# A streamed trunk of stick-breaking attention, sparse attention and two Strassen-style MLPs: second seed behind s3, its copies in tiles of their own, other times in the step planner, and x blocks through DRAM in 1 KB runs

## The chip, the core and the metric

The kernel runs on one core of a Trainium2 chip. The metric is the device time of one execution in microseconds (us): the median over the runs. TensorE (PE) multiplies, VectorE (DVE) and ScalarE (ACT) do elementwise work, GpSimd (POOL) and SyncE (SP) mainly issue DMAs here. All five run their own instruction streams in order and wait for one another through semaphores.

## The reference

256 tokens of width 2048 go through two residual layers; each is a mixer and then an MLP. What matters here is the MLP, which takes two thirds of the time:

```
for i in range(2):
    h = rms_norm(x, norm_mix[i])
    x = x + (stick_breaking_mixer(h, ...) if i == 0 else dsa_mixer(h, ...))
    h = rms_norm(x, norm_mlp[i])
    x = x + jnp.square(jax.nn.relu(h @ w_up[i])) @ w_down[i]     # 2048 -> 8192 -> 2048
```

All of it is float32. The mixers end in an output projection (out_proj) whose result is added to x.

## The kernel before, in words

**Weights and splits.** Weights stream from DRAM as blocks of 128 x 1024 float32 (256 rows of the matrix by 512 columns, 512 KB). Every block is one *item*. A load into a ring of six `wraw` tiles (L1777, queue of SP) is followed by a *split* into two float32r parts: ACT copies the block to `wh` (L1794), DVE subtracts it to get the rest `wl` (L1795). Each ring of parts has four tiles, so ACT may split an item once PE is done with the item four places earlier. The left operands are split likewise, and a product is the three partial products high x high, low x high, high x low: 12 matmuls for both token halves (a plain item, L855), or 6 for one half (a product of the set, L837).

**The MLP as pairs.** `mlp(l, next_col)` works on *pairs* of 512-column output groups, G and H. Each of the 16 pairs of a layer has eight weight blocks per column, and for all but the first (`up0`) four of the eight are replaced by two sets, a and b, of seven products each, in which sums of weight blocks (X, Y, Z, formed by DVE at L966, L969 and L978 and by a DMA that adds, issued by POOL at L973) meet sums of left blocks (`Sa`, `Sb` in the down pairs; the tile `Sx`, which the profile calls `half`, in the up pairs). So a pair is 14 products and 8 plain items, 14 x 6 + 8 x 12 = 180 matmuls. Their order on PE is written out: s1a . s1b s5a . s5b s6a s6b . s7a s7b s3a s3b . s2a s4a s2b s4b G0 G1 G2 G3; at the dots come the last items H0 to H3 of the pair before. 15 pairs of this kind run in each of the two MLPs, 30 in all.

**Seeds.** The products share sums. G's accumulator is a PSUM tile of two halves; s1, s6 and s7 add up in its second half. In `seeds(p, prior)` five small steps carry partial sums on: `first` (ACT, L1002) copies the second half to the first half of G after s1b; `second` (ACT, L1006) copies it to the first half of a tile U after s6b; `third` (ACT, L1009) copies it to the second half of U after s7b; `fourth` (DVE, L1013) opens the accumulator H and writes its first half, U subtracted from the product s5; `fifth` (DVE, L1016) writes its second half in the same way, and this is the **second seed**. s3a and s3b then add into H's first half, and H0 to H3 into both. The tile framework puts the waits in by whole tiles: a matmul into H waits for a write to H that stands before it in the program, whichever half it is.

**What sets the order of the side work.** The steps (seeds, sums, transposes, relu and square, DMAs) are put between the items by a planner, `Plan.run`, ahead of time. It walks over the items with costs written as numbers (A, V, MM for a split on ACT, on DVE and a matmul), with a latency per engine (`LAT`) and a latest start per step, and decides after which item each step is issued; the engines then run in that order. `done` holds a step back until an item has been issued, `needs` gives the item that must find it done.

**The way around DRAM.** A finished column of G or H is transposed by DVE in 32 x 32 blocks into a tile `y` (L926), written to DRAM by four DMAs (L934) and read back transposed (L942), in runs of 1 KB. At the end of a mixer, `add_residual` (L572) adds out_proj's result to x, and `turn` takes each of four x columns on a way of its own: L427 transposes, L435 writes in runs of 128 bytes, L440 reads, ACT (L471) and DVE (L476) form the high and low part of `xT`, the left operand of the MLP's first items. The places of these steps are fixed item counts (`later`).

Of the kernel before, what the change touches and what calls it, by code (L numbers as in the profile page):

```python
# [17 lines left out]
P = 128  # L18
# [24 lines left out]
NEAR = 5  # L43
DEEP = 3
ADD = True
# [49 lines left out]
class Plan:  # L95
# [3 lines left out]
    LAT = {"A": 0.25, "V": 0.25, "S": 2.6, "P": 3.5, "PE": 0.5}  # L99
    AHEAD = {"A": 1.2, "V": 2.0}  # L100

    def __init__(self, items, lead, bufs, raw):
        self.items, self.lead, self.bufs, self.raw = items, lead, bufs, raw
        self.steps = []
# [10 lines left out]
    def run(self, start, rings, extra=16):  # L115
# [30 lines left out]
        free = {"A": ideal[start], "V": ideal[start], "S": ideal[start]}  # L146
# [6 lines left out]
        self.own, self.loads = own, {}  # L153
        pe = ideal[start]
        late = 0.0

        def raw_free(k):
# [3 lines left out]
            t = lo.get(i)  # L161
# [51 lines left out]
        def place(s, i, t):  # L213
# [3 lines left out]
            if s.eng in "SP":  # L217
                b = max(free["S"], t)
                free["S"] = b + s.cost
                s.end = b + s.cost + self.LAT[s.eng]  # L220
            else:
                b = max(free[s.eng], t)
                s.end = free[s.eng] = b + s.cost
# [6 lines left out]
        for i in range(start, n + extra):  # L230
# [23 lines left out]
            while loaded < len(own):  # L254
# [32 lines left out]
            while more:  # L287
                more = False
                for s in todo[:60]:
# [6 lines left out]
                    else:  # L296
# [4 lines left out]
                        must = s.slot + late < pe + 1.5  # L301
                        if not must and (room < self.AHEAD[s.eng] or idle > 0.4
                                         and b > pe):
                            continue
# [21 lines left out]
def trunk(ctx, tc, x, x_t, gains_t, w_in_a, w_out_a, w_in_b, w_in_b_end, w_out_b, rel_bias, w_up, w_down, out):  # L326
# [92 lines left out]
    def turned(parts, whole=False, y=None):  # L419

        n = sum(part.shape[1] // P for part in parts)
        y = (tmp.tile([P, 8, P], F32, name="jx", bufs=3) if y is None else y)[:, :n, :]
# [36 lines left out]

    def turn_steps(c, col):  # L460
# [20 lines left out]
    def turn(c, col, wait):  # L481

        parts, high, low = turn_steps(c, col)

        def then(z):
            z = z.rearrange("p (t k) (a q) -> p t k a q", t=2, a=4)
# [3 lines left out]
        to_features(parts, any_tile, then, wait)  # L490
# [276 lines left out]
    def mlp(l, next_col):  # L767
# [119 lines left out]
        for i in range(6):  # L887
            add(up0, f"G{i}", f"H{i}")
        add(up0, "G6", "G7")
        before, tail = up0, ["H6", "H7"]  # L890
        for p in pairs:
            order = "s1a . s1b s5a . s5b s6a s6b . s7a s7b s3a s3b .".split()
            gaps = {4: (0, 1, 2, 3), 2: (1, 2)}[len(tail)]
            gap = 0
            for name in order:
                if name != ".":
                    add(p, name)
                    continue
                if gap in gaps:
                    add(before, tail.pop(0))  # L900
                gap += 1
            add(p, *"s2a s4a s2b s4b G0 G1 G2 G3".split())
# [15 lines left out]
        def turn(part, room):  # L918
            def f():
                if room.ring == "y":  # L920
                    room.tile = sec["pool"].tile([P, 4, 8, 32], F32, name="y", bufs=1)
                else:
                    room.tile = any_tile().rearrange("p n (b i) -> p (n b) i", b=4).rearrange(
                        "p (b n) i -> p b n i", b=4)
                for n, x in part():
                    keep(dve.transpose(room.tile[:, :, n, :], x.rearrange("p (k b i) -> p b k i",  # L926
                                                                          b=4, i=32)))
            return f

        def write(room):  # L930
            def f():
                room.d = drp.tile([4, 32, 4, 256], F32, name="tu", bufs=4)
                for a in range(4):
                    keep(nc.sync.dma_start(  # L934
                        room.d[:, :, a, :].rearrange("b j e -> j b e"),
                        room.tile[32 * a:32 * a + 32].rearrange("p b n i -> p b (n i)")))
            return f

        def read(room, d):
            def f():  # L940
                room.tile = any_tile().rearrange("p a e -> p (a e)")
                keep(nc.sync.dma_start(room.tile, d.d.rearrange("b j a e -> (b j) (a e)")))  # L942
            return f

        def by_token(z):
# [945 lines left out]
```

## Time and profile before

| | us |
|---|---|
| median of 3 runs (lowest, highest) | 2093.45 (2092.56, 2096.15) |
| the profiled execution, its own time | 2085.08 |
| its span, first to last instruction | 2083.4 |
| first mixer and the first items of the first MLP (0 to 416): PE busy | 413.9 |
| first MLP (416 to 1050): PE busy, DVE busy | 603.2, 563.2 |
| second mixer (1050 to 1404): PE busy | 354.0 |
| second MLP (1404 to 2084): PE busy, DVE busy | 644.7, 596.1 |

A row such as `wl<-wraw,wh` reads "tile written <- tiles read"; numbers of buffers are left out, so `acc` is any of the accumulators G and H, `aux` holds s5. Idle time of an engine that others do not wait for costs nothing; what has to be read is where PE stands, and what it stands for.

### The profile page before, as it was taken

To read this page: it belongs to the slowest core of one execution; us is meant where nothing else is said; L and a number is where in the kernel's file an instruction comes from. 1 tells how busy PE (TensorE), PEld (TensorE's weight loads), DVE (VectorE), ACT (ScalarE), POOL (GpSimd) and SP (SyncE) were. 2 spreads that over 40 slices of the span, in tenths; PEclk is the share of its full clock that TensorE was granted. 3 is DMA by queue.
4 is the path that set the end of the run, shared out by engine and by line. 5 is a ranking of instruction groups with operands and counts; after the bars stand their busy time and mean duration, and the time that the engine had idled before them with its cause. 6 is when DMAs were issued, how large, how long until landed. Compare 5 with 4: busy or idle time off the path is not lost. (4 is left out here: it accounts for less than half of the span.)

```text
span 2083.4 us, 25469 instructions
## 1 busy us (share of the span) xinstructions
PE 2015.8 (97%) x8858; PEld 1653.3 (79%) x8858; DVE 1747.8 (84%) x1921; ACT 1284.4 (62%) x1551; POOL 86.0 (4%) x131
## 2 busy tenths in 40 slices
PE   9999999999899999999999999999999999999999
PEld 7888888877777877887788788887777787778777
DVE  6779866799889889988885897669888898999886
ACT  6666655476566666666564566555666566676554
POOL 0000100002000000000000000000000000000000
PEclk9999999999999999999999999999999999999999
DMA  9777757878878877886677697587867788688774
GB/s 347 215 226 210 224 162 214 265 239 266 262 251 247 266 229 247 252 279 226 188 270 253 193 263 242 159 281 219 290 209 246 229 251 256 213 265 283 237 218 140
DMA packets 261537, 496.34 MB, mean 238 GB/s; under 512 B 121312, under 2 KB 150048, under 8 KB 261408
## 3 DMA queue, kind: packets, MB, share of 16 engines
q1 hardware_dynamic: 244720, 455.81, 66.1%
q0 software_dynamic: 8640, 31.46, 8.3%
q10 hardware_dynamic: 8048, 7.45, 1.1%
q8 instruction: 69, 1.13, 0.2%
q14 instruction: 60, 0.49, 0.1%
HBM read 457.36 MB, written 37.22 MB: 237 GB/s over the span
## 5 line engine op out<-in xcount | busy, mean ns | idle before, releaser
L1795 DVE TENSOR_TENSOR wl<-wraw,wh 128x1024 fp32r<-128x1024 f32 (+1 forms) x674 | 810.6, 1215 | 172.1 <-ACT wh L1794 162.5
L1794 ACT ACTIVATE wh<-wraw 128x1024 fp32r<-128x1024 f32 (+1 forms) x674 | 702.1, 1052 | 353.9 <-PE acc L855 111.4
L855 PE MATMUL acc<-wh,xT 128*128 128x512 f32 x1152 | 285.3, 390 | 2.8 <-DVE xT L476 2.8
L855 PE MATMUL acc<-wh,half 128*128 128x512 f32 x1016 | 256.4, 395 | 0.0
L855 PEld LDWEIGHTS acc<-wh,xT 128*128 128x128 f32 x1152 | 216.5, 188 | 48.5 <-DVE xT L476 3.4
L855 PEld LDWEIGHTS acc<-wh,half 128*128 128x128 f32 x1016 | 195.4, 192 | 41.7
L837 PE MATMUL acc<-wh,half 128*128 128x512 f32 x720 | 196.8, 396 | 16.3 <-DVE acc L1016 16.3
L558 PE MATMUL acc<-wh,xT 128*128 128x512 f32 x736 | 185.7, 392 | 0.0
L837 PEld LDWEIGHTS acc<-wh,half 128*128 128x128 f32 x720 | 136.3, 190 | 48.4 <-DVE acc L1016 19.7
L558 PEld LDWEIGHTS acc<-wh,xT 128*128 128x128 f32 x736 | 137.6, 188 | 30.0 <-issue 1.7
L855 PE MATMUL acc<-wl,xT 128*128 128x512 f32 x576 | 154.0, 389 | 0.0
L855 PE MATMUL acc<-wl,half 128*128 128x512 f32 x508 | 135.8, 389 | 0.0
L855 PEld LDWEIGHTS acc<-wl,xT 128*128 128x128 f32 x576 | 108.1, 188 | 22.5
L837 PE MATMUL acc<-wl,half 128*128 128x512 f32 x360 | 112.4, 394 | 1.7 <-DVE wl L1795 1.7
L855 PEld LDWEIGHTS acc<-wl,half 128*128 128x128 f32 x508 | 95.5, 188 | 20.0
L1794 ACT ACTIVATE wh<-Zb 128x1024 fp32r<-128x1024 f32 x60 | 63.3, 1056 | 63.2 <-PE acc L855 32.7
L558 PE MATMUL acc<-wl,xT 128*128 128x512 f32 x368 | 99.2, 391 | 0.0
L1795 DVE TENSOR_TENSOR wl<-Zb,wh 128x1024 fp32r<-128x1024 f32 x60 | 73.3, 1222 | 27.8 <-ACT wh L1794 27.0
L837 PE MATMUL acc<-wh,xT 128*128 128x512 f32 x336 | 89.8, 389 | 0.0
L837 PEld LDWEIGHTS acc<-wl,half 128*128 128x128 f32 x360 | 68.6, 191 | 16.7 <-DVE wl L1795 2.1
L558 PEld LDWEIGHTS acc<-wl,xT 128*128 128x128 f32 x368 | 68.9, 188 | 14.9 <-DVE wl L1795 0.3
L662 PE MATMUL acc<-wh,xT 128*128 128x512 f32 x320 | 79.7, 391 | 0.0
(296 smaller groups left out, 3022.1 us busy)
## 6 DMA issues: line engine op xcount, KB each, us to landing
wraw<-in_w_up_dram SPq DMA_DIRECT2D x228, 512.0 KB, 5.3
wraw<-in_w_down_dram SPq DMA_DIRECT2D x224, 512.0 KB, 5.0
wraw<-in_w_in_a_dram SPq DMA_DIRECT2D x88, 512.0 KB, 4.7
wraw<-in_w_in_b_dram SPq DMA_DIRECT2D x64, 512.0 KB, 4.6
jx<-tu SPq DMA_DIRECT2D x36, 512.0 KB, 6.2
wraw<-in_w_out_a_dram SPq DMA_DIRECT2D x32, 512.0 KB, 4.1
tu<-y SPq DMA_DIRECT2D x128, 128.0 KB, 4.0
wraw<-in_w_out_b_dram SPq DMA_DIRECT2D x32, 512.0 KB, 4.3
```

What stands on the lines that cost most here:

```text
L558: (keep if alone else pin)(pe.matmul(acc[t], L[:, KB * q + j, part, t * P:(t + 1) * P], wx[:, j, :], start=a and q == 0, stop=z and q == Q ...
L662: keep(pe.matmul(acc[:, t, :], L[:, KB * qs[i] + j, part, t * P:(t + 1) * P], wx[:, j, :], start=a and i == 0, stop=z and i == end - (last ...
L837: keep(pe.matmul(o, lhs(part, j), wx[:, j, :], start=a and opens, stop=z, skip_group_check=True))
L855: keep(pe.matmul(acc[:, t, :], L[:, KB * q + j, part, t * P:(t + 1) * P], wx[:, j, :], start=a and i == 0 and not self.sets, stop=z, skip_ ...
L1794: order(act.activation(wh[:, a], raw[:, a], AF.Copy))
L1795: order(dve.tensor_sub(wl[:, a], raw[:, a], wh[:, a].bitcast(F32)))
```

## The change

It has four parts.

1. **Seeds.** `fifth` also waits until s3b has been issued, so it stands behind s3 in the program. The copies of `second` and `third` go to tiles of their own, 128 x 512 from a ring of two, in place of two halves of one tile. `third` must be done by s2a, not by s4a.
2. **The planner's numbers.** Latencies are set to other values, SP's and POOL's transfers share one modelled set of DMA engines and have a time to issue each, and a step that reads what a DMA brings is not placed within 3 us (`SURE`) of the modelled landing unless it is due. The planner starts at item 4 of the MLP, not at item 8.
3. **x blocks.** `turn` uses the same layout as the MLP's columns: runs of 1 KB both ways. The fourth column's read and its two parts become steps of the planner (`last_column`), due at G6.
4. **The MLP's first items.** G0 H0 ... G4 H4 G5 G6 G7, with H5, H6, H7 at the dots of the next pair (before: up to H5 in turn, then G6 G7, with H6 and H7 at the dots).

The additions by DMA stay as they were (`ADD` is now a function that always answers True), as does every matmul, split and sum.

```
-ADD = True
+ADD = lambda p, s: True
...
-    LAT = {"A": 0.25, "V": 0.25, "S": 2.6, "P": 3.5, "PE": 0.5}
+    LAT = {"A": 1.5, "V": 2.0, "S": 2.0, "P": 3.0, "PE": 0.5}
+    SURE = 3.0
+    ISSUE = {"S": 0.33, "P": 1.2}
...
+        def transfer(queue, t, cost):
+            b = free[queue] = max(free[queue], t) + self.ISSUE[queue]
+            free["D"] = max(free["D"], b) + cost
+            return free["D"] + self.LAT[queue]
...
-                b = max(free["S"], f, pe - 10)
-                free["S"] = b + 1.5
-                landed[own[loaded]] = b + 1.5 + 2.6
+                landed[own[loaded]] = transfer("S", max(f, pe - 10), 1.6)
...
-                        if not must and (room < self.AHEAD[s.eng] or idle > 0.4
-                                         and b > pe):
+                        if not must and (room < self.AHEAD[s.eng] or idle > 0.4
+                                         and b > pe or b < landed_at + self.SURE):
...
     def turn(c, col, wait):
 
         parts, high, low = turn_steps(c, col)
+        y = y_view(any_tile())
+        for t in range(2):
+            turn_in(y, 4 * t, parts[t], lambda ins: None)
+
+        def write():
+            d = turn_write(y)
+            if c < 3:
+                later(3, read, d)
+            else:
+                handed.update(d=d, high=high, low=low)
...
-        to_features(parts, any_tile, then, wait)
+        later(1 + wait, write)
...
-        for i in range(6):
+        for i in range(5):
             add(up0, f"G{i}", f"H{i}")
-        add(up0, "G6", "G7")
-        before, tail = up0, ["H6", "H7"]
+        add(up0, "G5", "G6", "G7")
+        before, tail = up0, ["H5", "H6", "H7"]
...
             def second():
-                sec["U"] = sec["pool"].tile([P, 2, 512], F32, name="U", bufs=1)
-                keep(act.activation(sec["U"][:, 0, :], p.G[:, 1, :], AF.Copy))
+                p.two = sec["pool"].tile([P, 512], F32, name="U", bufs=2)
+                keep(act.activation(p.two, p.G[:, 1, :], AF.Copy))
 
             def third():
-                keep(act.activation(sec["U"][:, 1, :], p.G[:, 1, :], AF.Copy))
+                p.three = sec["pool"].tile([P, 512], F32, name="U", bufs=2)
+                keep(act.activation(p.three, p.G[:, 1, :], AF.Copy))
...
-            b = plan.step("A", 0.5, third, done(p, "s7b") + after(*prior.seed), needs("s4a"))
+            b = plan.step("A", 0.5, third, done(p, "s7b") + after(*prior.seed), needs("s2a"))
             a = plan.step("V", 0.6, fourth, done(p, "s5b") + after(a, prior.out["G"]), needs("s3a"))
-            p.seed = [a, plan.step("V", 0.6, fifth, after(a, b), needs("H0"))]
+            b = plan.step("V", 0.6, fifth, after(a, b) + done(p, "s3b"), needs("H0"))
+            p.seed = [a, b]
...
+        def last_column():
+
+            z = Room("jx")
+            b = plan.step("S", 1.5, read(z, lambda: handed["d"]), takes=z)
+            b = plan.step("A", 1.6, lambda: handed["high"](by_token(z.tile)), after(b), uses=[z])
+            plan.step("V", 2.1, lambda: handed["low"](by_token(z.tile)), after(b),
+                      [("mm", up0.by["G6"])], uses=[z])
...
-        for i, steps in plan.run(8, {"jx": 3, "y": 1}).items():
+        for i, steps in plan.run(4, {"jx": 3, "y": 1}).items():
```

Where the instructions stand is shown at three places of the first down pair, the third of the first MLP's 15 pairs, as each engine's program lists them (the times there are in the prediction). Numbers behind names tell tiles apart, `x3` stands for three alike, and the brackets name the engines whose semaphores an instruction waits for. Source lines of the changed kernel are some 30 to 45 higher: L1043 and L1046 are its fourth and fifth step, L882 and L900 its matmuls, L1835 its split on DVE.

PE before, from s3a (on `Sa`) over s3b (on `Sb`) to the plain item; `acc_4289` is H:

```order
L837 MATMUL acc_4289<-wh_4273,Sa_3136 128x512 [waits DVE_49,PE_49,Activation_49]
L837 MATMUL acc_4289<-wh_4273,Sa_3136 128x512 x3
L837 MATMUL acc_4289<-wl_4274,Sa_3136 128x512 x2
L837 MATMUL acc_4289<-wh_4293,Sb_3140 128x512 [waits DVE_49]
L837 MATMUL acc_4289<-wh_4293,Sb_3140 128x512 x3
L837 MATMUL acc_4289<-wl_4294,Sb_3140 128x512 x2
```

and the same place of the changed kernel, where H is `acc_4290`:

```order
L882 MATMUL acc_4290<-wh_4269,Sa_3148 128x512 [waits DVE_49,PE_49,Activation_49]
L882 MATMUL acc_4290<-wh_4269,Sa_3148 128x512 x3
L882 MATMUL acc_4290<-wl_4270,Sa_3148 128x512 x2
L882 MATMUL acc_4290<-wh_4294,Sb_3152 128x512 [waits Activation_49]
L882 MATMUL acc_4290<-wh_4294,Sb_3152 128x512 x3
L882 MATMUL acc_4290<-wl_4295,Sb_3152 128x512 [waits DVE_49]
```

The matmuls are the same; the first one of s3b no longer waits for DVE, only for ACT's part of its own weights.

DVE before, from the fourth step (L1013) to the split behind the fifth (L1016), at the same place:

```order
L1013 TENSOR_TENSOR acc_4289<-aux_4171,U_4266 128x512 [waits DVE_49]
L1795 TENSOR_TENSOR wl_4294<-wraw_4101,wh_4293 128x1024 [waits PE_49,Activation_49]
L978 TENSOR_TENSOR Za_3139<-Za_3139,wraw_4122 128x1024 [waits DMAHW5_49]
L1795 TENSOR_TENSOR wl_4307<-wraw_4103,wh_4306 128x1024 [waits DMAHW4_49,PE_49,Activation_49]
L1795 TENSOR_TENSOR wl_4319<-wraw_4122,wh_4318 128x1024 [waits PE_49,Activation_49]
L1016 TENSOR_TENSOR acc_4289<-aux_4171,U_4266 128x512 [waits PE_49,Activation_49]
L1795 TENSOR_TENSOR wl_4331<-Za_3139,wh_4330 128x1024 [waits Activation_49]
```

and of the changed kernel, where the fifth step is L1046:

```order
L1043 TENSOR_TENSOR acc_4290<-aux_4174,U_4265 128x512 [waits DVE_49]
L1007 TENSOR_TENSOR Za_3151<-Za_3151,wraw_4142 128x1024 [waits DMAHW6_49]
L1835 TENSOR_TENSOR wl_4295<-wraw_4107,wh_4294 128x1024 [waits PE_49,Activation_49]
...
L473 STREAM_TRANSPOSE y_4409<-acc_3909 128x1024 [waits DMAHW5_49,DMAHW6_49,DMAHW4_49,DMAHW3_49]
L1835 TENSOR_TENSOR wl_4412<-wraw_4337,wh_4411 128x1024 [waits DMAHW2_49,PE_49,Activation_49]
L995 TENSOR_TENSOR Xa_3149<-Ya_3150,wraw_4349 128x1024 [waits DMAHW3_49]
L1046 TENSOR_TENSOR acc_4290<-aux_4174,U_4317 128x512
```

The fifth step went from 5 rows behind the fourth to 17 rows behind it, past the next pair's first sum, and it waits for no other engine there. In the whole program it stands at 18 of 30 places with waits for PE and ACT before, and at 5 with a wait for PE now.

DVE at the start of the same pair before, where the low part of the left sum Sb (L1116) is formed:

```order
L969 TENSOR_TENSOR Za<-Xa,wraw 128x1024
L1795 TENSOR_TENSOR wl<-Xa,wh 128x1024
L1795 TENSOR_TENSOR wl<-wraw,wh 128x1024
L1101 TENSOR_TENSOR jx<-jx 128x2x4x32
L1102 TENSOR_TENSOR jx<-jx 128x2x4x32
L1103 TENSOR_TENSOR jx<-jx 128x2x4x32
L1104 TENSOR_TENSOR jx<-jx 128x2x4x32
L969 TENSOR_TENSOR Zb<-Xb,wraw 128x1024
L1795 TENSOR_TENSOR wl<-Xb,wh 128x1024
L1795 TENSOR_TENSOR wl<-Za,wh 128x1024
L1116 TENSOR_TENSOR Sb<-jx,Sb 128x1024
```

and of the changed kernel (L998 is L969, L1147 is L1116):

```order
L998 TENSOR_TENSOR Za<-Xa,wraw 128x1024
L1835 TENSOR_TENSOR wl<-wraw,wh 128x1024
L998 TENSOR_TENSOR Zb<-Xb,wraw 128x1024
L1835 TENSOR_TENSOR wl<-Xb,wh 128x1024
L1147 TENSOR_TENSOR Sb<-jx,Sb 128x1024
L1835 TENSOR_TENSOR wl<-Za,wh 128x1024
```

The four sums (L1101 to L1104) now stand ahead of this place, and the low part comes four rows behind Za, not ten.

More of the change, by code (lines that the diff above doesn't have):

```diff
@@ L43 @@
 NEAR = 5
+ORDER = "s1a . s1b s5a . s5b s6a s6b . s7a s7b s3a s3b . s2a s4a s2b s4b G0 G1 G2 G3"
 DEEP = 3
-ADD = True
+ADD = lambda p, s: True
 LEAD = 2
@@ L153, in run @@
         self.own, self.loads = own, {}
+        self.held = {index(a): index(b) for a, b in self.hold}
         pe = ideal[start]
         late = 0.0
+        def transfer(queue, t, cost):
+            b = free[queue] = max(free[queue], t) + self.ISSUE[queue]
+            free["D"] = max(free["D"], b) + cost
+            return free["D"] + self.LAT[queue]
         def raw_free(k):
@@ L160, in raw_free @@
             i = own[k - self.raw]
-            t = lo.get(i)
+            t = lo.get(self.held.get(i, i))
             if t is None:
@@ L301, in run @@
                         must = s.slot + late < pe + 1.5
+                        landed_at = max([x.end for kind, x in s.after
+                                         if kind == "step" and x.eng in "SP"] + [0.0])
                         if not must and (room < self.AHEAD[s.eng] or idle > 0.4
-                                         and b > pe):
+                                         and b > pe or b < landed_at + self.SURE):
                             continue
@@ L417, in later, with turned @@
         due[clock[0] + n].append(lambda: f(*a))
[L419 removed]
+    def turned(parts, whole=False):
         n = sum(part.shape[1] // P for part in parts)
[L422 removed]
+        y = tmp.tile([P, 8, P], F32, name="jx", bufs=3)[:, :n, :]
         m = 0
@@ L885, in add @@
             items.extend(p.by[name] for name in names)
-        for i in range(6):
+        for i in range(5):
             add(up0, f"G{i}", f"H{i}")
-        add(up0, "G6", "G7")
-        before, tail = up0, ["H6", "H7"]
+        add(up0, "G5", "G6", "G7")
+        before, tail = up0, ["H5", "H6", "H7"]
         for p in pairs:
[L892 to L895, printed above, removed]
+            for name in ORDER.split():
                 if name != ".":
                     add(p, name)
-                    continue
-                if gap in gaps:
+                elif tail:
                     add(before, tail.pop(0))
-                gap += 1
-            add(p, *"s2a s4a s2b s4b G0 G1 G2 G3".split())
             before, tail = p, [f"H{i}" for i in range(4)]
@@ L931, in f @@
             def f():
[L932 to L936, printed above, removed]
+                room.d = turn_write(room.tile)
             return f
```

62 lines of the change are left out of this document (38 added, 24 removed).

## The prediction

> **What bounds the kernel now.** I began with the page's busy shares and then asked for the waits of PE, since an engine that is busy for nearly the whole span can only be made faster where it stands. Rows of waits read "engine line waited for: us in total, times, longest us".
>
> ```profile
> PE 2015.8 (97%) x8858; PEld 1653.3 (79%) x8858; DVE 1747.8 (84%) x1921; ACT 1284.4 (62%) x1551; POOL 86.0 (4%) x131
> core 0: 2083.4 us, clock 0.989
> PE acc L837 <- DVE acc L1016: 39.6, 18, 3.1
> PE aux L837 <- DVE Sb L1116: 10.1, 4, 2.9
> PE aux L837 <- DVE half L1116: 4.9, 2, 2.7
> PE acc L855 <- DVE xT L476: 2.8, 1, 2.8
> PE acc L837 <- DVE wl L1795: 1.7, 1, 1.7
> PE aux L837 <- ACT Sb L1112: 0.9, 2, 0.5
> ```
>
> PE is idle for 2083.4 - 2015.8 = 67.6 us, and 39.6 us of that are 18 waits of about 2.2 us for the second seed. The clock row holds a second loss: a mean of 0.989 is 0.011 x 2083.4 = 22.9 us in which PE is called busy but runs slower.
>
> What such a wait is made of stands in the timeline of the first down pair (start, length, engine, line):
>
> ```profile
> 519.50 0.61 PE L837 MATMUL acc<-wl,Sb 128*128 128x512 f32 x2
> 519.95 1.07 PE L837 MATMUL acc<-wh,Sa 128*128 128x512 f32 x4
> 520.42 2.35 DVE L1795 TENSOR_TENSOR wl<-wraw,wh 128x1024 fp32r<-128x1024 f32 x2
> 520.67 0.57 ACT L1009 ACTIVATE U<-acc 128x512 f32<-128x512 f32 x1
> 520.86 0.61 PE L837 MATMUL acc<-wl,Sa 128*128 128x512 f32 x2
> 522.70 0.69 DVE L1016 TENSOR_TENSOR acc<-aux,U 128x512 f32<-128x512 f32 x1
> 523.44 1.20 PE L837 MATMUL acc<-wh,Sb 128*128 128x512 f32 x4 [1.97 <-DVE acc L1016]
> L1016 DVE TENSOR_TENSOR acc<-aux,U x30: 668/693/695, 441.4 to 2054.9; 128x512 f32<-128x512 f32 x30
> ```
>
> The first row ends s7b at 520.11; s3a ends at 521.47. The seed, which waits for it, starts behind two splits at 522.70, and s3b starts when the seed is done, though it writes the other half of H. Of 30 seeds 18 make PE wait. In the listing of the program before, the same number, 18, stand between s3a and s3b, with a wait for PE on them; the other 12 stand behind s3b and made PE wait nowhere. So the kernel itself holds the comparison that I need.
>
> The last view is busy time by stretches. Columns after the bounds: length, then busy us (and instructions) of PE, PEld, DVE, ACT, POOL, then granted clock, DMA share, GB/s. First seven stretches around waits for the seed, then four between them that hold no wait of PE, and the sum of these and of one more:
>
> ```profile
> 739.00:749.00 10.00, 7.70 (x27) 6.21 (x28) 6.96 (x7) 3.39 (x4) 0.00 (x0) 0.83 0.66 237
> 951.00:961.00 10.00, 7.19 (x20) 5.37 (x19) 6.59 (x7) 2.70 (x4) 0.00 (x0) 0.66 0.72 241
> 1001.00:1011.00 10.00, 8.16 (x29) 6.23 (x29) 7.18 (x8) 4.02 (x6) 0.00 (x0) 0.83 0.71 225
> 1568.00:1578.00 10.00, 7.41 (x25) 5.95 (x26) 7.18 (x7) 3.36 (x4) 0.00 (x0) 0.83 0.69 229
> 1612.00:1622.00 10.00, 8.09 (x29) 6.19 (x28) 7.19 (x8) 4.14 (x5) 0.00 (x0) 0.83 0.67 220
> 1657.00:1667.00 10.00, 7.88 (x29) 6.05 (x28) 6.12 (x7) 6.58 (x8) 0.00 (x0) 0.83 0.75 283
> 1954.00:1964.00 10.00, 7.64 (x27) 5.82 (x26) 7.18 (x7) 3.48 (x5) 0.00 (x0) 0.83 0.67 238
> ...
> 664.00:734.00 70.00, 70.00 (x310) 57.97 (x310) 64.02 (x61) 44.61 (x47) 3.46 (x4) 1.00 0.80 248
> 834.00:950.00 116.00, 116.00 (x513) 96.08 (x512) 106.74 (x99) 77.92 (x82) 5.21 (x6) 1.00 0.84 259
> 1664.00:1740.00 76.00, 76.00 (x337) 62.92 (x336) 67.91 (x65) 49.10 (x50) 3.47 (x4) 1.00 0.79 239
> 1835.00:1951.00 116.00, 116.00 (x513) 96.08 (x512) 106.13 (x99) 78.09 (x81) 5.21 (x6) 1.00 0.82 257
> sum 438.00, PE 437.95 PEld 362.16 DVE 398.74 ACT 292.26 POOL 20.81; mean PE 87.59 PEld 72.43 DVE 79.75 ACT 58.45 POOL 4.16
> ```
>
> Two readings. Behind seven of the 18 waits the clock drops, by 0.17 of 10 us in six stretches and 0.34 in one. And where PE isn't held up it runs at full clock for 116 us on end, while DVE is busy 398.74 of 438 us, 91%. The second bound is therefore DVE, with 9% to spare, and it bears PE's full pace.
>
> **The change part by part.** The sum is made against the profiled execution, 2085.1 us, which is its span and 1.7 us around it. The median of the runs, 2093.45, is 8.4 us above that; I carry these 8.4 us over to the result whole, since no row says what they are.
>
> *Second seed behind s3: the waits.* All 30 seeds now stand behind s3b, most of them 9 to 18 rows later on DVE, and are due only at H0, behind s2, s4, G0 to G3 and s1a of the next pair. The work is the same, 0.69 us each, and it lies in DVE's 9%. Gain: 39.6 us. For five of the 30 the listing shows a wait for PE at the seed: there DVE, an engine that works in order, stands until s3b is done, and the splits behind it with it. In the 12 cases before, none of this reached PE. I price it at zero, and what it costs if it does is in the rivals.
>
> *The clock behind them.* 6 x 0.17 x 10 + 0.34 x 10 = 13.6 us at the profile's clock; it goes with the waits. [...]
>
> *Getting going again.* A pair of 180 matmuls takes 15 x 2.72 us = 40.8 us undisturbed, by the first of these rows; between the other two lies one pair, with a wait of 2.12 us:
>
> ```profile
> 1528.45 2.72 PE acc L855 x12
> 785.44 1.19 PE L837 MATMUL acc<-wh,half 128*128 128x512 f32 x4 [1.44 <-DVE acc L1016]
> 828.65 1.19 PE L837 MATMUL acc<-wh,half 128*128 128x512 f32 x4 [2.12 <-DVE acc L1016]
> ```
>
> 43.21 - 40.80 - 2.12 = 0.29 us more than the idle time. For 18 waits 5.2 us.
>
> *Copies in tiles of their own, third step due at s2a.* No instruction is added. The copy at 520.67 is done at 521.24, 1.1 us after s7b's end. s2a follows behind s3a and s3b, six matmuls and so 1.36 us each, in most pairs with a plain item between, so the copy has at least 2.7 us. Zero, on ACT, which is busy 62%; if ACT is late by more than 1.6 us the wait is on PE (rivals).
>
> *The planner's numbers: the left sums.* Four waits for Sb, two for the same sum in the up pairs (`half`) and two short ones for ACT's part make 10.1 + 4.9 + 0.9 = 15.9 us; the clock loss that the seeds don't explain, 22.9 - 13.6 = 9.3 us, can only lie behind these and the three single waits; eight restarts are 2.3 us. Together 27.5 us. Will they go? On DVE:
>
> ```profile
> 499.13 1.23 DVE L969 TENSOR_TENSOR Za<-Xa,wraw 128x1024 f32<-128x1024 f32 x1 [2.12 <-DMA wraw<-in_w_down_dram]
> 507.66 1.22 DVE L1116 TENSOR_TENSOR Sb<-jx,Sb 128x1024 fp32r<-128x1024 f32 x1
> 508.93 1.03 PE L837 MATMUL aux<-wh,Sb 128*128 128x512 f32 x3 [2.95 <-DVE Sb L1116]
> ```
>
> Sb's low part starts 8.5 us after Za before. In the changed listing it comes four rows after it, and at the 1.14 us from one such row to the next (two in 2.35 us above) that is 4.6 us. It gains 3.9 us, against 0.47 + 2.95 = 3.4 us that PE stood there. That is enough by half a microsecond, if Za is not later itself. For `half` the low part now comes ahead of Za by some rows, which leaves several us. The bounds are nothing and all; I take three quarters, 20.6 us, since the Sb case is near the edge.
>
> *x blocks and first items.* The longer runs touch 16 writes of 128 KB ahead of each MLP. Their landing hardly differs: rows of issues, with us to landing at the end.
>
> ```profile
> td<-jx SPq DMA_DIRECT2D x96, 128.0 KB, 4.2
> tu<-jx SPq DMA_DIRECT2D x16, 128.0 KB, 4.3
> 1412.01 2.18 DVE L476 SCALAR_TENSOR_TENSOR xT<-jx,gains,xT 128x128 fp32r<-128x128 f32 x8
> ```
>
> So the layout by itself is worth nothing; of its effect on the 2.8 us wait at G6 only the place matters. The low part stands 8 splits behind the last transposes in the changed listing, 11 before, and at 2.72 us an item that is 8.2 us earlier than 1412.0. G6 is 2.72 us earlier too. I count the 2.8 us as gone and half of the 1.9 us of waits for splits (1.7 and 0.2): 3.7 us, from bounds of 0 and 4.7.
>
> *New waits.* Steps were moved all over both MLPs, and a full-speed PE leaves no slack. No row shows these waits. From below they are 0; I charge three at 2.2 us with one clock drop of 1.7 us, 8.3 us, and half as much again for the range.
>
> *Sum.* 39.6 + 13.6 + 5.2 + 20.6 + 3.7 - 8.3 = 74.4 us. 2085.1 - 74.4 = 2010.7 for a profiled execution, and 2093.45 - 74.4 = **2019** us for the median.
>
> **The rivals.**
>
> *Raw loads take it back.* DVE already stands for loads that its sums read:
>
> ```profile
> DVE Za L969 <- DMA wraw<-in_w_down_dram: 21.6, 9, 5.9
> DVE Zb L969 <- DMA wraw<-in_w_down_dram: 9.7, 8, 1.8
> ```
>
> One such wait of 5.9 us came through to PE as the wait for a split of 1.7 us. If at full pace half of the 30 pairs had one of 1.7 us, with a clock drop behind every second, that is 15 x 1.7 + 7 x 1.7 = 37.4 us, and the time 2019 + 37 = 2056. Against it stand the four undisturbed stretches, with a DMA share of 0.79 to 0.84.
>
> *The wait moves to s2a.* If third runs late, PE stands at s2a in place of s3b. At 1 us in 18 pairs and 0.29 each, 23 us are given back: 2042. ACT's 62% speaks against it.
>
> *The clock drops stay,* if they come from something other than the waits: 13.6 and three quarters of 9.3 are not gained, 2019 + 20.6 = 2040. [...]
>
> *Slower: DVE becomes the bound.* A pair takes 40.8 us of PE and 0.91 x 40.8 = 37.1 us of DVE. From 3.7 us of standing per pair on, in-order DVE sets the pace, and each further us costs 30 us in all. The change must give back 74.4 us to lose, 2.5 us per pair, so it takes 6.2 us of standing per pair; at 7 us the time is 2019 + 30 x 3.3 = 2118. Seeds that wait for s3b with the splits queued behind would be the place. Only five seeds have that wait, and the waits for raw loads above are about 1 us per pair.
>
> *Nothing happens,* because s3b waits for something else that is as late. The 12 pairs without the wait speak against it: 2093.
>
> **How the numbers follow.** About 0.2%, 4 us, can be told from no change. The chances: forecast 0.80; raw loads 0.09; s2a 0.03; clock 0.03; nothing 0.02; slower 0.03. Faster is 0.80 + 0.09 + 0.03 + 0.03 = 0.95, same 0.02, slower 0.03. The range's low end takes all of the left sums (27.5), all of the single waits (4.7) and no new waits: 58.4 + 27.5 + 4.7 = 90.6, 2003, and 8 us less, as the runs' distance to the profile may shrink with the waits: 1995. Its high end takes the seeds' three terms alone less one and a half times the new waits: 58.4 - 12.5 = 45.9, 2048. That also holds the rivals of s2a and the clock.
>
> **What would show it.** Right: no wait of PE for the line of the second seed (L1046 there), and a pair in 40.8 to 41.5 us; the mean clock at 0.995 or above; the waits for Sb and `half` short or gone; DVE busy 92 to 95% of the two MLPs. Wrong: waits of PE for splits (`wl`), for a copy (`U`) or at s2a in their place, DVE standing for raw loads by more than now, or a clock that still drops in undisturbed stretches.

## The result, and the profile after the change

The changed kernel takes 2006.45 us (median of 4 runs, 2006.12 to 2006.96) against 2093.77 us (4 runs, 2092.56 to 2096.15) for the kernel before: a ratio of 0.9582, 95% interval 0.9565 to 0.9598. The forecast was 2019 us, from 1995 to 2048. The profiled execution took 2006.96 us.

The page of the changed kernel, the busy time of the engines (share of the span, instructions):

```profile
PE 1991.1 (99%) x8858; PEld 1640.1 (82%) x8858; DVE 1738.5 (87%) x1921; ACT 1281.4 (64%) x1551; POOL 93.4 (5%) x131
```

PE was idle for 67.6 us before and is idle for 2005.2 - 1991.1 = 14.1 us now: 53.5 us less. It is also busy for 24.7 us less, with the same 8858 matmuls. Most of that is the clock: by the mean granted clock of the two profiles, 24.0 us of the span were lost to it before and 2.8 us now, 21.2 us less (0.9885 and 0.9986 before rounding). The other 3.5 us are the remainder, which I put down to getting going again behind waits (0.29 us for the one taken apart in the prediction). Idle and busy time together make 78.2 us, the difference of the spans. The clock (core, span, mean granted clock):

```profile
core 0: 2005.2 us, clock 0.999
```

What PE still waits for (engine, line, waited for: us in total, times, longest us):

```profile
PE aux L882 <- DVE wl L1835: 3.6, 4, 1.8
PE acc L900 <- DVE wl L1835: 1.5, 3, 1.1
PE aux L882 <- DVE Sb L1147: 1.4, 3, 0.6
...
PE acc L882 <- DVE wl L1835: 0.5, 1, 0.5
```

Nothing waits for the second seed (L1046) any more; 39.6 us are gone whole. The left sums went from 15.9 to 1.4 us, xT from 2.8 to nothing. Waits for splits (wl) went up from 1.9 to 3.6 + 1.5 + 0.5 = 5.6 us. Sum: -39.6 - 14.5 - 2.8 + 3.7 = -53.2 of the 53.5 us.

The views by stretch (columns as in the prediction), first of 327 us in the first MLP, then of the middle of both MLPs with their sum:

```profile
602.00:929.00 327.00, 327.00 (x1445) 270.75 (x1444) 308.46 (x294) 220.63 (x229) 13.88 (x16) 1.00 0.83 262
...
480.00:1000.00 520.00, 516.46 (x2266) 425.63 (x2265) 484.62 (x467) 350.56 (x365) 39.94 (x57) 1.00 0.83 263
1420.00:1960.00 540.00, 539.12 (x2377) 445.52 (x2376) 509.82 (x489) 369.21 (x382) 22.59 (x26) 1.00 0.82 260
sum 1060.00, PE 1055.58 PEld 871.15 DVE 994.44 ACT 719.77 POOL 62.52; mean PE 527.79 PEld 435.58 DVE 497.22 ACT 359.89 POOL 31.26
```

For 327 us PE doesn't stand at all: 1445 matmuls at 180 per pair are 8.03 pairs of 40.7 us. But DVE is busy for 994.44 of 1060 us, 93.8%, or 38.3 us of a pair of 40.8, where the prediction had 37.1.

The new waits are for splits, which DVE forms. Here is what DVE waits for at the sums that stand ahead of them, in the changed kernel:

```profile
DVE Za L998 <- DMA wraw<-in_w_up_dram: 18.3, 10, 4.6
DVE Za L998 <- DMA wraw<-in_w_down_dram: 16.3, 10, 4.7
DVE Xa L995 <- DMA wraw<-in_w_up_dram: 7.2, 2, 4.5
DVE Zb L998 <- DMA wraw<-in_w_up_dram: 5.7, 3, 2.4
DVE Zb L998 <- DMA wraw<-in_w_down_dram: 5.6, 7, 2.2
```

With two smaller rows that is 57.5 us at the loads of the weight ring, against 39.9 before; the kernel before has another 4.2 us for the DMA that adds, the changed one none. In the profile of the changed kernel's second set of runs (below) it is 49.7 us. How the longest reaches PE stands in the timeline (start, length, engine, line, in brackets the idle time before it):

```profile
539.07 1.23 DVE L998 TENSOR_TENSOR Za<-Xa,wraw 128x1024 f32<-128x1024 f32 x1 [4.67 <-DMA wraw<-in_w_down_dram]
540.21 1.22 DVE L1835 TENSOR_TENSOR wl<-Xa,wh 128x1024 fp32r<-128x1024 f32 x1
541.48 0.74 PE L882 MATMUL aux<-wl,Sa 128*128 128x512 f32 x2 [1.83 <-DVE wl L1835]
542.05 3.54 PE L900 MATMUL acc<-wh,half 128*128 128x512 f32 x8
```

The sum Za stands 4.67 us for a load; the split behind it in DVE's order is late, and PE waits 1.83 us for it. Then eight matmuls take 3.54 us; elsewhere, from 566.79 for one, eight of the same kind take 1.98 us. That is the one place inside the MLPs where the clock still drops: 0.50 from 542.13 to 545.54 us.

### The profile page after: what moved, and what is told of

Read it like the earlier page. It is cut to its first block, busy times and chain, and to the rows that moved or that the text cites. A ratio compares the mean times of both kernels' runs of the same rounds, so it can differ in the third digit from the quotient of the medians.

```text
span 2005.2 us, 25492 instructions
## 1 busy us (share of the span) xinstructions
PE 1991.1 (99%) x8858; PEld 1640.1 (82%) x8858; DVE 1738.5 (87%) x1921; ACT 1281.4 (64%) x1551; POOL 93.4 (5%) x131
## 4 chain that ended last, share of the span: by engine, by line
PE 93%; DVE 3%; DMA 2%; issue 1%; ACT 0%; SPq 0%; DVEq 0%; ACTq 0%
PE acc L900 33%; PE acc L882 23%; PE acc L603 21%; PE acc L707 5%; PE aux L882 4%; PE aux L726 2%; DVE wl L1835 2%; PE acc L726 1%; DMA wraw<-in_w_down_dram 1%; DMA wraw<-in_w_up_dram 1%; PE aux L1698 1%; PE acc L594 0%; PE acc L1372 0%; PE aux L1432 0%; PE acc L1586 0%
## 5 line engine op out<-in xcount | busy, mean ns | idle before, releaser
L1835 DVE TENSOR_TENSOR wl<-wraw,wh 128x1024 fp32r<-128x1024 f32 (+1 forms) x674 | 808.6, 1215 | 126.4 <-ACT wh L1834 117.8
L900 PE MATMUL acc<-wh,xT 128*128 128x512 f32 x1152 | 284.7, 389 | 0.0
L900 PEld LDWEIGHTS acc<-wh,xT 128*128 128x128 f32 x1152 | 216.2, 188 | 45.2
L900 PE MATMUL acc<-wh,half 128*128 128x512 f32 x1016 | 252.5, 391 | 0.0
L900 PEld LDWEIGHTS acc<-wh,half 128*128 128x128 f32 x1016 | 191.6, 189 | 40.0
L882 PE MATMUL acc<-wh,half 128*128 128x512 f32 x720 | 192.9, 390 | 0.0
L882 PEld LDWEIGHTS acc<-wh,half 128*128 128x128 f32 x720 | 134.8, 188 | 29.3 <-ACT wh L1834 0.6
L900 PE MATMUL acc<-wl,xT 128*128 128x512 f32 x576 | 154.5, 390 | 0.6 <-DVE wl L1835 0.4
L900 PE MATMUL acc<-wl,half 128*128 128x512 f32 x508 | 136.0, 389 | 1.1 <-DVE wl L1835 1.1
L900 PEld LDWEIGHTS acc<-wl,xT 128*128 128x128 f32 x576 | 107.8, 188 | 24.5 <-DVE wl L1835 2.3
L900 PEld LDWEIGHTS acc<-wl,half 128*128 128x128 f32 x508 | 95.5, 188 | 21.4 <-DVE wl L1835 1.5
L882 PE MATMUL acc<-wl,half 128*128 128x512 f32 x360 | 111.0, 390 | 0.5 <-DVE wl L1835 0.5
L882 PE MATMUL acc<-wh,xT 128*128 128x512 f32 x336 | 89.8, 389 | 0.0
L1834 ACT ACTIVATE wh<-Za 128x1024 fp32r<-128x1024 f32 x60 | 63.4, 1056 | 31.2 <-DVE Za L998 19.0
L882 PEld LDWEIGHTS acc<-wl,half 128*128 128x128 f32 x360 | 67.4, 188 | 15.0 <-DVE wl L1835 1.1
```

The lines of the kernel that those rows point to most:

```text
L882: keep(pe.matmul(o, lhs(part, j), wx[:, j, :], start=a and opens, stop=z, skip_group_check=True))
L900: keep(pe.matmul(acc[:, t, :], L[:, KB * q + j, part, t * P:(t + 1) * P], wx[:, j, :], start=a and i == 0 and not self.sets, stop=z, skip_ ...
L1834: order(act.activation(wh[:, a], raw[:, a], AF.Copy))
L1835: order(dve.tensor_sub(wl[:, a], raw[:, a], wh[:, a].bitcast(F32)))
```

## The experiments

The theory and its rivals are those of the prediction. Medians are compared with the kernel before on the same chip.

**The seed alone.** The kernel before, with one condition more:

```
-            p.seed = [a, plan.step("V", 0.6, fifth, after(a, b), needs("H0"))]
+            p.seed = [a, plan.step("V", 0.6, fifth, after(a, b) + done(p, "s3b"), needs("H0"))]
```

> Only the condition that puts the second seed behind s3b, on the kernel before. In the listing 0 of 30 seeds then stand between s3a and s3b (18 before). The theory (what counts is where the seed stands): the 18 waits, 39.6 us, the clock behind them, 13.6 us, and the restarts, 5.2 us, go, and the waits for the left sums (15.9 us and their clock) stay: ratio (2093.8 - 58.4) / 2093.8 = 0.972, some 2035 us. The rival that a wait only moves to another place: half of that at most, 2065 us or more.

Measured: 2038.27 us against 2086.12 (ratio 0.9748, 0.9716 to 0.978). Waits of PE in it:

```profile
PE aux L837 <- DVE Sb L1116: 11.3, 4, 2.9
PE aux L837 <- DVE wl L1795: 3.2, 5, 1.0
PE acc L837 <- DVE wl L1795: 3.1, 1, 3.1
PE aux L837 <- DVE half L1116: 3.0, 2, 2.3
PE acc L855 <- DVE xT L476: 2.5, 1, 2.5
PE acc L837 <- ACT U L1006: 1.6, 2, 1.3
```

The row of the seed (L1016) is gone; no wait of its size takes its place. The left sums stay, 11.3 + 3.0 = 14.3 us against 15.0 in the same two rows before. This one condition accounts for more than half of the result.

**The planner's numbers alone.** The kernel before with the new class Plan (LAT, SURE, ISSUE, the shared DMA engines) and the seed without its condition.

```
-    LAT = {"A": 0.25, "V": 0.25, "S": 2.6, "P": 3.5, "PE": 0.5}
+    LAT = {"A": 1.5, "V": 2.0, "S": 2.0, "P": 3.0, "PE": 0.5}
+    SURE = 3.0
+    ISSUE = {"S": 0.33, "P": 1.2}
```

> Only the planner's new numbers, on the kernel before. The listing shows that they alone take 11 to 13 of the 18 seeds out from between s3a and s3b. The theory (the place counts, whichever edit sets it): 13 x 3.2 us = 42 us of the seeds' share, and the waits for the left sums with their clock, 15.9 + 9.3 + 2.3 = 27.5 us: some 2024 us. The rival that the seed's own condition is what matters: only the left sums, 2066 us.

Measured: 2045.93 us (ratio 0.9785, 0.9749 to 0.982). Against the kernel before on this chip that is 40 us less, where 69.5 were expected. Waits of PE:

```profile
PE acc L843 <- DVE acc L1022: 22.2, 7, 4.1
PE acc L861 <- DVE xT L482: 5.1, 2, 3.5
...
PE aux L843 <- DVE Sb L1122: 1.1, 2, 0.7
```

The left sums fall to 1.1 us, or 1.9 with 0.8 for `half`, so these numbers suffice to remove them. They also put 11 of the 18 seeds behind s3b without being told to. The seven that stay cost 3.2 us each, not 2.2: in four of them a sum and a split of DVE start between the end of s3a and the seed, where the kernel before had splits alone, two at most. The wait got rarer and longer.

**All but the seed's condition, and all but the planner's numbers.** The changed kernel with one part taken back. For the first:

```
-            b = plan.step("V", 0.6, fifth, after(a, b) + done(p, "s3b"), needs("H0"))
+            b = plan.step("V", 0.6, fifth, after(a, b), needs("H0"))
```

> The changed kernel without the seed's condition (5 to 7 seeds stand between s3a and s3b again). The theory: 5 to 7 waits of 2.2 us return, with 0.29 us each to get going again and the clock behind half of them: 16 to 23 us more, 2022 to 2029 us. The rival that the condition is what matters: 58 us more, 2065 us.

For the second the class Plan of the kernel before is put in:

> The changed kernel with the planner's old numbers (no seed between s3a and s3b). The theory: the waits for the left sums and for late splits return, up to 27.5 us, so up to 2034 us; since the x blocks and the first items are new, the waits of the first pair may stay away (a third of it), 2025 us. The rival that the numbers are worth little once the seeds are moved: within 8 us of the changed kernel, 2014 us at most.

Measured: 2033.49 us without the condition (0.9725, 0.9694 to 0.9757), and 2023.97 with the old numbers (0.9674, 0.9636 to 0.9713). The first has the same seven seeds, at 20.8 us:

```profile
PE acc L882 <- DVE acc L1046: 20.8, 7, 4.1
```

The second has left sums again, and ACT's copy of s6's sum, `second` of the seeds, for which the next matmuls into G wait:

```profile
PE aux L876 <- DVE Sb L1141: 6.5, 3, 2.9
PE acc L876 <- ACT U L1029: 5.8, 4, 3.2
```

The first is 4 us above the range expected of it, the second 1 us below its own. The two parts overlap: the condition is worth 48 us alone and 2033.5 - 2005.5 = 28 us on top of the rest; the numbers 40 us alone and 18 on top of the rest. Here 2005.5 us is about where the two sets of runs of the changed kernel lie (2006.45, and 2005.17 below), on other chips than these four runs. Only 7 of 18 seeds need the condition once the planner is right. With the planner's old numbers 6.5 us of the left sums remain, not all 15.9; another part of the change removes the rest as well, as the run with the x blocks shows.

**The copies alone.** The kernel before with two tiles for the copies and `third` due at s2a:

```
-                sec["U"] = sec["pool"].tile([P, 2, 512], F32, name="U", bufs=1)
-                keep(act.activation(sec["U"][:, 0, :], p.G[:, 1, :], AF.Copy))
+                p.two = sec["pool"].tile([P, 512], F32, name="U", bufs=2)
+                keep(act.activation(p.two, p.G[:, 1, :], AF.Copy))
```

> The kernel before with the copies of the second and third step in tiles of their own, the third due at s2a, and nothing else: 18 of 30 second seeds stay between s3a and s3b. Forecast's theory: worth nothing by themselves; 18 waits for the second seed of 35 to 42 us in all, clock 0.983 to 0.990, time within 0.4% of the kernel before (2083 to 2100 us). Rival: the tile of two halves was itself a cause of the waits, since a copy into one half waits for the reader of the other; then the waits fall by a third or more, by 13 us, with the clock behind them by 4 us, and the time is 2070 to 2078.

Measured: 2090.46 us against 2093.63, ratio 0.9988 (0.9972 to 1.0004): no change that could be told. The seeds stand as they did:

```profile
PE acc L837 <- DVE acc L1017: 39.1, 18, 3.4
```

**The x blocks and the first items.** First by themselves on the kernel before: the layout in runs of 1 KB, the fourth column as steps of the planner, the items up to G4 H4 in turn, and the planner's start at item 4.

```
-        for i in range(6):
+        for i in range(5):
             add(up0, f"G{i}", f"H{i}")
-        add(up0, "G6", "G7")
-        before, tail = up0, ["H6", "H7"]
+        add(up0, "G5", "G6", "G7")
+        before, tail = up0, ["H5", "H6", "H7"]
```

> Only the x blocks in 1 KB runs, the fourth column as planner steps and the new order of the first items, on the kernel before. The theory: of this only the 2.8 us wait at G6 and at most the first pair's 2.3 to 2.7 us waits per layer count, so 2 to 10 us less than the kernel before. The rival that the shorter run of packets helps the whole kernel: 15 us or more.

Then the other way round, all of the change but these:

> The kernel before with three of the change's parts and not the rest: the second seed behind s3b, the copies in tiles of their own, and the planner's numbers. The x blocks and the order of the first items are as before. Forecast's theory: the x blocks and the first items are worth about 4 us, so 2009 to 2011 us; the wait for xT at G6 (2.5 to 5.1 us in the runs with the old blocks) is there, and otherwise only short waits. Rival, by the run that had the x blocks alone and came out 14.7 us below the fastest of the shared times, at the same clock: they are worth 10 to 15 us also here, and this kernel takes 2016 to 2022 us. A third: they are worth nothing now, 2004 to 2007.

Measured: by themselves 2080.49 us (ratio 0.993, 0.9899 to 0.9961), 14.8 us below the kernel before, with six runs from 2068.69 to 2083.53. (The second expectation takes this for the distance to the fastest run of the kernel before; that one is 3.8 us above.) Without them the median is 2014.89 (2014.35 to 2018.19; 0.9641, 0.9612 to 0.967), 8.4 to 9.7 us above the changed kernel, between what the theory and the rival had. What PE waits for in the kernel with these alone:

```profile
PE acc L876 <- DVE acc L1039: 44.6, 20, 3.4
PE acc L876 <- ACT U L1029: 4.5, 2, 3.0
PE aux L876 <- DVE Sb L1139: 4.2, 2, 2.1
```

The wait for xT is gone, and so are four of the six longer waits for left sums (15.9 us before, 4.2 here), though the planner's numbers are the old ones. Two more seeds stand in the way, and ACT's copy is late twice. The profiled executions are 3.6 us apart (2081.51 against 2085.08) and the medians 14.8, which is above the 2 to 10 us of the theory and just short of the rival's 15. Two rows of what PE waits for in the kernel without them:

```profile
PE acc L861 <- DVE xT L482: 5.0, 2, 3.0
PE aux L843 <- DVE wl L1802: 3.3, 4, 2.3
```

By the profiled executions it is 2016.5 - 2005.2 = 11.3 us longer, of which PE's idle time is 7.2 and its busy time, at a clock of 0.997 instead of 0.999, is 4.1. The forecast said 3.7 us. The wait for xT at G6 is the largest part. It is 2.8 us before and 2.5 with the seed's condition alone, but 5.1 with the planner's numbers alone and 5.0 here, so its growth goes with those numbers and not with the pace. How much these parts are worth by themselves is not settled closer than the interval, and which of them removes the left sums no run takes apart.

**The changed kernel again, and DVE's reserve.** The changed kernel was run a second time beside two variants, in which DVE does a sum twice, into the same tile: X only (2 x 1.14 us per pair at the spacing of such rows), or X and Z. The planner isn't told, so the order is that of the changed kernel.

```
                 def t1(R=R, by=by):
                     keep(dve.tensor_add(R["X"], R["Y"], raw_of(by["s1"])))
+                    keep(dve.tensor_add(R["X"], R["Y"], raw_of(by["s1"])))
```

> The changed kernel once more, beside the three others of this call on the same chip. Both theories: 2006 us within 2 us, mean clock 0.999, since hardly a wait is left that could slow the clock, while the kernel before scatters by 10 us or more with its clock.

> The changed kernel with the first weight sum (X) formed twice in both sets, the same values: 2 more instructions of 1.14 us on DVE per pair, 2.3 us in 30 pairs. The theory that DVE has some 9% or 3.7 us per pair to spare: nearly hidden, up to 10 us more (2006 to 2016 us). The rival that DVE is already the bound at PE's full pace: 30 x 2.3 = 68 us more, 2075 us.

> The changed kernel with X and the second sum (Z) formed twice in both sets: 4.6 us more on DVE per pair. The theory of a reserve of 3.7 us: 0.9 us per pair is too much, 27 us, and waits with the clock behind them some more: 2033 to 2050 us. The rival that DVE is already the bound: 30 x 4.6 = 137 us, 2143 us. If DVE had much more to spare than its busy share says: 2006 us.

Measured: 2005.17 us (2003.59 to 2005.64) for the changed kernel, 2035.86 (2033.63 to 2038.15) with X twice, and 2108.18 (2107.4 to 2110.74) with both twice, which is slower than the kernel before: ratio 1.0069, 1.0043 to 1.0095. The pages of the two, first X:

```profile
PE 2003.9 (98%) x8858; PEld 1635.4 (80%) x8858; DVE 1808.5 (89%) x1981; ACT 1275.9 (63%) x1551; POOL 95.2 (5%) x131
```

then X and Z:

```profile
PE 2021.7 (96%) x8858; PEld 1638.9 (78%) x8858; DVE 1881.5 (89%) x2041; ACT 1274.7 (61%) x1551; POOL 85.1 (4%) x131
```

DVE's busy time of the second run of the changed kernel was 1739.5 us. X adds 69.0 us, 2.3 per pair, and the time rises by 30.7, 1.0 per pair; both add 142.0, 4.7 per pair, and cost 103.0, 3.4 per pair. Both say the same: the first 1.3 us per pair are free, and each further us is paid whole (the times hold some loss of clock too, 2.3 us and 11.6 us in the two profiles). The stretches say why. Sums over the middle of the MLPs, X first (490 to 1020 and 1440 to 1990):

```profile
sum 1080.00, PE 1060.78 PEld 862.42 DVE 1049.55 ACT 711.10 POOL 63.77; mean PE 530.39 PEld 431.21 DVE 524.78 ACT 355.55 POOL 31.89
```

and X and Z (490 to 1040 and 1470 to 2050):

```profile
sum 1130.00, PE 1062.67 PEld 854.28 DVE 1097.87 ACT 703.73 POOL 54.25; mean PE 531.34 PEld 427.14 DVE 548.93 ACT 351.87 POOL 27.12
```

DVE is busy for 97.2% in both, and doesn't get beyond it here. 0.972 x 40.8 = 39.7 us of a pair can be used, and 38.3 are: 1.4 us to spare, which fits the 1.3 from the times. Both results are far above what the forecast's reserve gave, by 20 and by 58 us. What PE waits for with X and Z twice:

```profile
PE aux L882 <- DVE wl L1837: 31.4, 26, 2.1
PE acc L900 <- DVE wl L1837: 18.6, 21, 2.2
PE aux L882 <- DVE Sb L1149: 12.9, 4, 3.2
PE acc L882 <- DVE wl L1837: 11.9, 21, 1.1
```

That is 68 waits for splits, most of them short, and the left sums. This is how the forecast's rival of the other sign looks.

**A later place for the sums.** A version: the rule of 3 us behind a modelled landing also counts the loads of the weight ring, which X and Z read.

```
                         landed_at = max([x.end for kind, x in s.after
-                                         if kind == "step" and x.eng in "SP"] + [0.0])
+                                         if kind == "step" and x.eng in "SP"] + [
+                                             landed[index(x)] for kind, x in s.after
+                                             if kind == "raw"] + [0.0])
```

> The changed kernel, in which the planner's rule of 3 us behind a modelled landing (SURE) also counts the loads of the weight ring (wraw), which the sums X and Z read. Theory: what eats VectorE's reserve in the changed kernel is that it stands in order at these sums for loads that have not landed: 18.3 + 16.3 + 7.2 + 5.7 + 5.6 us, some 53 us in all or 1.8 us per pair. If the rule moves the sums behind the landings, the standing falls below 25 us, the waits of TensorE for splits (5.6 us) below 2 us, and the time to 2000 to 2003 us from 2005 to 2006. Rival: the sums are then late for the splits that read them, as they have nowhere else to go; the standing is moved to TensorE as waits of 2 to 3 us for wl behind Za or Xa, and the time is 2010 or more. No difference (2004 to 2007) would say that the modelled landing is not where loads land.

> The same kernel as in the run with the landings of the weight ring counted (2001.31 us, 1996.66 to 2005.61), to see whether its 4 us below the changed kernel (8 runs from 2003.6 to 2007.0) are its own. If so, the median is 1999 to 2004 us and most runs are below 2003.6, TensorE's waits for splits and sums come to less than 5 us, and its idle time to 9 to 11 us. If the lower runs were chance, the median is 2004 to 2007. VectorE's standing at loads stays at 40 us or more in both cases, as it did in the first run (20.0 + 16.8 + 3.6 + 2.9 us), so that the gain then does not come from less standing but from where it falls.

Measured: 2001.31 us (1996.66 to 2005.61, 4 runs), and on another chip 2000.31 (1999.03 to 2002.95, 5 runs; ratio to the kernel before 0.9575, 0.9556 to 0.9594). The changed kernel's eight runs, not beside it, go from 2003.59 to 2006.96. So it is 5 us less by the times, on different chips, and by the profiles 10.7 and 10.2 us of idle time of PE against 14.1 and 13.3; the ratios to the kernel before (0.9572 and 0.9575, against 0.9582 and 0.9574) are too coarse to tell the two apart. What PE waits for at the left sums and splits of the MLPs, in the second profile:

```profile
PE aux L884 <- DVE Sb L1149: 2.6, 4, 0.9
...
PE acc L902 <- DVE wl L1837: 0.2, 1, 0.2
PE aux L884 <- DVE wl L1837: 0.2, 1, 0.2
```

and DVE's longest standing at loads:

```profile
DVE Za L1000 <- DMA wraw<-in_w_up_dram: 14.5, 9, 3.7
DVE Zb L1000 <- DMA wraw<-in_w_down_dram: 11.8, 9, 3.6
```

The waits for splits fell from 5.6 and 5.1 us in the two profiles of the changed kernel to 1.8 and 0.4, as the theory had it. The standing at loads fell too, but only in part: with two more rows each, from 57.5 and 49.7 us to 43.3 and 36.2, where the first expectation had less than 25 and the second 40 or more. How much of the gain comes from it is open. The steps moved all over both MLPs, and which of the moves keeps the splits on time is not settled.

## Why the prediction was right, and where it failed

**The seeds (39.6 us): right.** The row is gone, and the seed's condition alone removes it. DVE stood idle ahead of none of the 30 seeds of the changed kernel, the five with a wait for PE included.

**The clock behind the waits (13.6) and getting going again (5.2): right in kind.** With the left sums' part (8.7), 27.5 us were expected to go from PE's busy time, less 1.7 for a new drop: 25.8. 24.7 went. Of the two terms the clock was set too low, 18.9 us against 21.2, and the restarts too high, 6.9 against 3.5: they were read off a single pair. The rival that the clock drops for another reason is refuted: the mean clock went to 0.999, and it is between 0.993 and 0.997 in the profiled executions of the kernels without one of the three parts that count, or with only one of the two main ones.

Not every wait has a drop behind it, as two of the kernel before of the same length show, 2.12 and 2.11 us:

```profile
828.65 1.19 PE L837 MATMUL acc<-wh,half 128*128 128x512 f32 x4 [2.12 <-DVE acc L1016]
...
989.55 0.50 PE L837 MATMUL aux<-wh,Sb 128*128 128x512 f32 x1 [2.11 <-DVE Sb L1116]
```

In the clock records of this profile a drop is a stretch of 3.41 us at a clock of 0.50 (once two on end; the last, behind all matmuls, is recorded for 2.14 us), and all 14 records of a drop begin on one grid of 3.413 us, to within 4 ns over the whole span. For each of the two waits, here are the window of this grid that holds most of it and the window behind it, the clock third from the end:

```profile
827.14:830.55 3.41, 1.90 (x8) 1.60 (x9) 2.58 (x3) 2.90 (x4) 0.00 (x0) 1.00 1.01 407
830.55:833.96 3.41, 3.41 (x16) 2.83 (x16) 1.93 (x2) 2.19 (x3) 0.00 (x0) 1.00 0.43 123
...
987.57:990.98 3.41, 1.43 (x6) 1.22 (x7) 3.41 (x4) 3.38 (x5) 0.00 (x0) 1.00 0.00 0
990.98:994.39 3.41, 3.41 (x9) 2.65 (x9) 2.99 (x4) 3.38 (x4) 0.00 (x0) 0.50 0.45 115
```

The border of two windows cuts the first wait into 0.61 and 1.51 us, and the clock stays. Of the second, 1.98 us lie in one window, and the next one runs at half clock: 9 matmuls in place of 16, 1.7 us lost. The wait of the changed kernel for the split at 541.5 us is, in its first profile, 1.83 us long, all in one window of that profile's grid, and followed by a drop (0.50). In its second profile it is 2.24 us long:

```profile
542.02 0.50 PE L882 MATMUL aux<-wl,Sa 128*128 128x512 f32 x1 [2.24 <-DVE wl L1835]
...
538.07:541.48 3.41, 1.71 (x8) 1.09 (x6) 1.87 (x2) 0.53 (x1) 0.00 (x0) 1.00 1.05 278
541.48:544.89 3.41, 2.87 (x13) 2.37 (x14) 2.57 (x3) 1.01 (x2) 0.00 (x0) 1.00 0.95 327
```

1.70 us of it lie in the first of these two stretches and 0.54 us in the second, and the clock is 1.00 in both; where the grid of this profile lies, no row shows. In the profile of the kernel before, between the first and the last matmul, PE was idle for more than 1.94 us of 11 windows of the grid at full clock, and the next window is at 0.50 each time. Of the six in which it was idle for 1.82 to 1.94 us, two are followed by a drop; of those with less, none. Of the 26 waits over 1.4 us in this profile, 13 have a drop within 8 us.

**The 8.4 us between median and profile: wrong.** They were carried over whole, as no row said what they are. The rows of runs say it: the kernel before goes from 2082.2 us at a clock of 0.990 to 2101.2 at 0.983 in the runs of this study, and the changed kernel from 2003.6 to 2007.0 at 0.999 to 1.000. 0.007 of 2090 us is 14.6 us, most of that scatter. The profiled execution of before, at 0.989, was one with few drops. The offset was clock, which the change takes away; after it, the median is 0.5 us below the profiled execution. This step makes 8.4 + 0.5 = 8.9 us of the 12.6 by which 2019 was too high.

**The left sums: right cause, too small.** Three quarters were counted, 11.9 us of waits; 14.5 went. The planner's numbers remove them, as the run with these alone shows; but the x blocks, the first items and the planner's earlier start take 11.7 us of them by themselves as well, and the prediction credits these parts with none of it.

**The x blocks and the first items: the wait for xT went as said,** 2.8 us. On top of the rest they are worth more than the 3.7 us counted, 8 to 11 us: the planner's new numbers make that wait longer, 5.0 us, where these parts are missing.

**New waits: right place, too dear.** 6.6 us of waits and 1.7 of clock were charged without a row. There were 3.7 us more for splits, with one drop. Against the forecast's sum of 74.4 the 78.2 us measured come out so: 2.6 more from the left sums, 2.0 from the waits for splits, new and old, 0.3 from the other waits, 1.1 less from clock and restarts. The rival of the raw loads works this way (the 4.67 us at Za, then the split, then PE), but all waits for splits together took 5.6 us, not 37.4. Two signs that the prediction lists for being wrong did appear, waits for `wl` and DVE standing longer for raw loads, and neither was large enough to undo it.

**DVE's reserve of 3.7 us per pair: wrong.** The step took DVE's 91% from stretches that hold no wait of PE. In the four that it shows, DVE had less to do than on average, which may be why PE didn't wait there: 37.1 us to 180 matmuls, while the middle of both MLPs before (490 to 1030 and 1470 to 2040) has 984.31 us of DVE to 4551 matmuls, 38.9 us to 180. Over whole pairs of the changed kernel DVE needs 38.3 us, not 37.1. And it took the rest to 100% as usable, where two kernels stop at 97.2%. The reserve is 1.3 us. DVE's busy share of the MLPs, 92 to 95% expected, is 93.8% in their middle, and 93.2% and 92.0% from end to end (416 to 1050, 1360 to 2005). The kernel stayed on the good side of the bound by 1.3 us of a pair, and the chance of 0.03 for the slower rival rested on a margin that was not there. That nothing went wrong at this step was luck.

**Copies, third at s2a: right,** no wait at s2a and no gain. ACT's copies do make PE wait where other parts of the change meet the planner's old numbers, 5.8 us in four waits with all the rest of the change, 4.5 us in two with the x blocks alone, 2.8 us in three with the seed's condition alone, but not in the kernel before. With the new numbers, and no work added to DVE, it is 0.3 us at most.

## What to carry to other kernels

When one accumulator is written by a small step in the middle of a row of matmuls, ask which matmuls have to come before it and put it behind all that don't; here one condition was worth 48 us of 2090. A stretch in which the bounding engine never waits is a biased sample of the next engine's load: take whole periods, and measure the reserve by adding work. If a kernel's runs scatter with the granted clock, as they did here (0.982 to 0.991 in the kernel before), expect the distance from its profile to its median to go with the waits. And don't price a wait by its length alone: of two of 2.12 and 2.11 us here, one had no drop of the clock behind it, the other had one that cost 1.7 us.

## What the runs showed of the hardware

Short waits cost no clock here. The kernel with X and Z twice has 2106.2 - 2021.7 = 84.5 us of idle time and a clock of 0.995; the kernel before has 67.6 us and 0.989. In the profiles of these two, of the one with X twice and of the one with the copies alone, none of the 30 waits of PE from 1.4 to 1.8 us has a drop of the clock within 8 us behind it. Of those of 1.8 us and more, 13 of 23 do in the kernel before, 12 of 23 with the copies alone, and 5 of 6 with X and Z twice. So the drops did not go with the sum of idle time. In the kernel before they went with how much of it fell into one window of the grid of 3.413 us that its clock records show: over 1.94 us in 11 windows at full clock, with a drop behind each, and under 1.82 us without one. A wait of less can't fill a window that far by itself, and a longer one did or didn't by where it fell, which would fit the scatter of that kernel's runs, at clocks of 0.982 to 0.991. What settles the six windows in between stays open; PE's idle time is known only as well as the profile models the ends of matmuls.
